# Layer 0's output projection: six pairs of tiles by seven half-size block products, the residual by accumulating DMAs, and copies put behind stores

## The chip, the cores and the metric

The kernel runs on one core of a Trainium2 chip. A core has TensorE (PE, matmuls; PEld is its weight load), VectorE (DVE), ScalarE (ACT), GpSimd (POOL) and SyncE (SP, which here only starts DMAs); ACT and POOL can start DMAs too, and each engine takes its instructions in order. Sixteen DMA engines move the data. The metric is the device time of one execution in microseconds (us), lower is better.

## The reference

Two layers of a diffusion backbone work on 2304 tokens of 1024 features: 256 context tokens (two tiles of 128) and 2048 latent ones (sixteen tiles). Layer 0 is even (latent attention and gated linear attention side by side), layer 1 is odd (neighbourhood attention on a grid of width 64). Cut to what matters here:

```python
def even_mixer(...):
    ...
    def readout(a, b, za, zb):
        a = a.reshape(bsz, n, A_WIDTH) * jax.nn.silu(za)
        b = rms_norm(b, gla_gain).reshape(bsz, n, B_WIDTH) * jax.nn.silu(zb)
        return jnp.dot(jnp.concatenate([a, b], axis=-1), w_out)

def reference(...):
    for i in range(DEPTH):
        shift, scale, gate = modulation(c, ada_w[i], ada_b[i])
        h = rms_norm(x, norm_g[i]) * (1 + scale) + shift
        ...
        y, yc = even_mixer(...) if i % 2 == 0 else odd_mixer(...)
        x = x + gate * y
        if update_ctx:
            cx = cx + c_gate * yc
    return x
```

The change touches `jnp.dot(..., w_out)` of layer 0, a product of 2304 x 1024 by 1024 x 1024, and the sum `x + gate * y` behind it. All is fp32.

## The kernel before

An fp32 product is made of three matmuls of rounded halves: each operand is split into a high part (rounded to the matmul's type fp32r, by ACT) and a low part (the rest, by DVE), and high·high, high·low and low·high are added up in PSUM. A matmul has a 128x128 block of activations as its stationary operand and a 128x512 block of weights as its moving one; a tile of 128 tokens against 1024x1024 weights takes 8 blocks of k, 2 halves of the columns and 3 products, 48 matmuls.

The stages, with their stretches in the trace of before: even_latent and even_rest (0 to 1100 us; layer 0's input products, even_rest storing its columns as Un and zaT with POOL's DMAs), even_mix (1100 to 1895 us; attention and gated linear attention, their readout stored as RT, transposed), layer 0's output projection (1895 to 2093), odd_qk and odd_vz (2093 to 3004; layer 1's input products, cell by cell: a cell is a tile t against 512 columns j of w_od), layer 1's attention (3004 to 3400), and layer 1's output projection (to the end). Tiles of SBUF come from pools with a fixed number of buffers per tag (`bufs`), and an instruction that writes a buffer waits for the last reader of its former content. The order on each engine is set by a scheduling layer from the data's dependences and the order of the code; `issue_after(x)` puts what stands in it behind x on its engine.

The projection is `project`, called by even_mix. For each tile it loads RT (pr, 512 KB) and xin (px, 512 KB) by SP (`project_load`), splits pr into prh and prl (`project_split`), runs 48 matmuls into two banks pj (`project_steps`), multiplies each bank by the gate (DVE, py, L1284), adds the residual on POOL (px<-py,px, L1288), and stores the tile to x1 in DRAM by SP. The weights w_out0 lie in SBUF, split, in places that earlier stages have left: D0 to D13, gu, gqt, gkt, gkT, gat, tri, woh/wol and gG. Between tiles, the generator `ahead` makes steps of the next stage: the splits of w_od's columns j = 2 and 3 (w0h/w0l, w1h/w1l, `od_steps`) and the preps of tiles 0 and 1 of layer 1, which read x1, normalise and transpose it (8 PE transposes, L339) and scale it to hT.

odd_qk goes over the cells in the order of `cells`: the first two tiles together (0,2), (1,2), (0,3), (1,3), then tile by tile; tile t + 2's prep is made when a tile has had its last cell. The weights of j = 0 and 1 (w2h/w2l and w3h/w3l, L106 and L391) are loaded and split beside the first four cells. odd_vz stores silu(z) as z1 (z<-ozt, ACT's DMA, L1453) and copies x1's latent tiles to the output in DRAM (out_dram<-x, 16 copies of 512 KB, ACT's queue, L1455); since these wait for x1 alone, the schedule had them earlier, from 1941.7 to 2098.0 us.

Layer 1's output projection (L1826 on) has the scheme that the change brings to layer 0: tiles 0 to 3 plain, then six pairs by seven products of half size (`seven`, matmuls at L1940), the results added to the output by POOL's accumulating DMAs (L1960).

Of the kernel before, what the change touches and what calls it, by code (L numbers as in the profile page):

```python
# [88 lines left out]
class Kern:  # L89
# [236 lines left out]
    def transposed(self, t, src, pp, tag, xp=None):  # L326

        nc, sp = self.nc, self.prp
        x = self.tl(xp or sp, [P, D], "x", bufs=1)
# [44 lines left out]
    def split_steps(self, dst, key, wp, src, K, cols, tag, step, rows=None, stage=None, place=None):  # L374
# [8 lines left out]
        for k0 in range(0, K, step):  # L383
            s = slice(k0, min(k0 + step, K))
            for c0 in range(0, cols, width):
# [3 lines left out]
                if rows is None:  # L389
                    self.act(hi[:, s, c], w[:])  # L390
                    nc.vector.tensor_tensor(out=lo[:, s, c], in0=w[:], in1=hi[:, s, c], op=ALU.subtract)  # L391
                    continue
# [8 lines left out]
    def even_latent(self, ws, wrest, kept):  # L401
# [6 lines left out]
        with ExitStack() as es:  # L408
# [3 lines left out]
            with ExitStack() as es2:  # L412
                st = self.pool(es2, "adaS", side="left", reuse_waits="tile")
                rows = self.transposed(0, self.i["xin"], pp, px, st)
# [192 lines left out]
    def even_rest(self, ws, win, hT):  # L607
        nc = self.nc
        self.zaT = self.scr("zaT", (4, P, T), F32)
        with ExitStack() as es:  # L610
# [5 lines left out]
            def cell(t, j):  # L616
# [547 lines left out]
    def even_mix(self, e1, win, hT):  # L1164
        nc = self.nc
        self.RT = self.scr("RT", (KD, P, T), F32)
        self.x1 = self.scr("x1", (T, D), F32)
        with ExitStack() as es:
            with ExitStack() as esa:
# [31 lines left out]
                def side():  # L1201
# [11 lines left out]
                    pre[0] = self.project_load(self.RT, 0, self.i["xin"], ld)  # L1213
                    yield "unit"
                    yield "unit"
                    r, x = pre[0]
                    hi, lo = self.tl(ld, [P, KD, P], "prh", F32R, bufs=1), self.tl(ld, [P, KD, P], "px", F32R)
                    self.project_split(r[:], hi[:], lo[:])
                    pre[0] = hi, lo, r, x
# [9 lines left out]
            def ahead():  # L1229
                for j in (2, 3):  # L1230
                    yield from self.od_steps(win, j, ws)
                for t in range(2):
                    hT[t] = self.prep(1, t, self.x1, pp, ("pj", 4))
                    yield
                    yield

            u = 2 * KD - 1
            self.split_unit(w, u, self.load_unit(u, self.tl(sp, [P, 512], "py")), [self.tl(g1, [P, 512], "gG", F32R, bufs=2)[:] for _ in range(2)])
            gate = [self.gate_load(0, c, self.tl(sp, [P, D], f"gate{c}", bufs=1)[:]) for c in range(2)]
            self.project(self.RT, range(NT), self.i["xin"], self.x1, w, sp, pp, pre["ld"], pre, gate, ahead())  # L1240
# [17 lines left out]
    def project_load(self, RT, t, xsrc, ld):  # L1258
# [3 lines left out]
        x = self.tl(ld, [P, D], "px")  # L1262
        self.nc.sync.dma_start(x[:], xsrc[t * P : t * P + P, :])
        return r, x
# [5 lines left out]
    def project_steps(self, hi, lo, x, g, w, bank, y, dst, split=KD):  # L1270
# [4 lines left out]
        for n, k0, k1 in runs:  # L1275
            c = slice(n * 512, n * 512 + 512)
            if k0 == 0:
                ps[n] = bank()
            yield from self.mm3_steps(ps[n][:], (lambda k: hi[:, k, :], lambda k: lo[:, k, :]),
                                      (lambda k: w[k, n][0][:, 0, :], lambda k: w[k, n][1][:, 0, :]), range(k0, k1), k0 == 0, k1 == KD)  # L1280
# [10 lines left out]

    def gate_load(self, l, c, g):
# [3 lines left out]
    def project(self, RT, tiles, xsrc, dst, w, sp, pp, ld, pre, gate, ahead):  # L1296

        for t in tiles:
            if t in pre:
                hi, lo, r, x = pre.pop(t)  # L1300
            else:
                hi, lo = [self.tl(sp, [P, KD, P], "pr" + c, F32R)[:] for c in "hl"]
                r, x = self.project_load(RT, t, xsrc, ld)
                self.project_split(r[:], hi, lo)
# [798 lines left out]
```

## Time and profile before

| what | us |
|---|---|
| time, median of three runs (lowest to highest) | 3562.49 (3561.96 to 3566.05) |
| profiled execution, its own time | 3569.04 |
| its span | 3567.2 |
| output projection of layer 0, first to last matmul | 1895.11 to 2092.97 |
| start of odd_qk, to its first full stretch | 2092.97 to 2135.64 |
| TensorE busy, share of the span | 3465.4, 97% |
| mean granted clock of TensorE | 0.987 |

A row of the timeline or of a chain is start, length, engine and operation, `out<-in` by the program's tile names. In grouped rows a bar stands ahead of busy time, mean duration in ns, and the idle time just before with what ended it. A window's row gives, for each engine, busy us and in brackets the number of instructions. Matmuls overlap: one lasts 0.39 us and they start 0.227 us apart.

### The profile page before, as it was taken

How to read it: one execution, taken by the hardware profiler on the slowest of the kernel's cores; microseconds unless marked ns; L12 is line 12 of the kernel's file. 1: busy time of each engine (PE TensorE's matmuls, PEld its weight loads, DVE VectorE, ACT ScalarE, POOL GpSimd, SP SyncE). 2: the span in 40 equal slices, each digit the busy share in tenths (PEclk: the TensorE clock that was granted, in tenths of full speed). 3: DMA queues.
4: the chain of work that ended last, by engine and by line, in shares of the span. 5: the costliest groups of instructions: out<-in, count | busy, mean ns of one | idle time of the engine just before them, and what ended most of it. 6: DMA issues, size and time to landing. Idle time of an engine off the chain costs nothing.

```text
span 3567.2 us, 54003 instructions
## 1 busy us (share of the span) xinstructions
PE 3465.4 (97%) x19532; PEld 2680.1 (75%) x19532; DVE 2400.1 (67%) x4709; ACT 1419.3 (40%) x2562; POOL 1248.8 (35%) x1382
## 2 busy tenths in 40 slices
PE   7999998999999999999999999999899999999999
PEld 6888987888896666665557878888788887555577
DVE  4677655888885777768874345545577784666775
ACT  5454552111113455446653124444422223555532
POOL 1333431100101333322212233333334443888842
PEclk9999999999999999999999999999999999999999
DMA  7555554222215242334526654445744447888675
GB/s 252 150 155 161 148 144 137 72 87 76 86 52 153 64 132 79 110 111 139 169 82 210 212 174 134 139 144 167 234 146 127 145 121 189 214 218 223 188 213 92
DMA packets 377292, 521.52 MB, mean 146 GB/s; under 512 B 34153, under 2 KB 253753, under 8 KB 370866
## 3 DMA queue, kind: packets, MB, share of 16 engines
q1 hardware_dynamic: 329762, 418.42, 40.7%
q0 software_dynamic: 24096, 63.26, 6.8%
q10 hardware_dynamic: 23168, 36.38, 2.9%
q8 instruction: 155, 2.54, 0.3%
q14 instruction: 111, 0.91, 0.1%
HBM read 338.62 MB, written 187.69 MB: 148 GB/s over the span
## 4 chain that ended last, share of the span: by engine, by line
PE 80%; DMA 7%; DVE 6%; ACT 2%; POOL 2%; issue 2%; SPq 1%; DVEq 0%; ACTq 0%; POOLq 0%
PE st L1130 10%; PE gm L129 10%; PE gm L130 10%; PE gm L131 10%; PE av L1040 7%; PE mx L660 4%; PE o L1624 2%; PE st L1590 2%; DMA wraw<-w_od 2%; PE pj L129 2%; PE pj L131 2%; PE pj L130 2%; PE o L1940 2%; DMA adaw<-ada_w 1%; PE st L1940 1%
## 5 line engine op out<-in xcount | busy, mean ns | idle before, releaser
L661 DVE TENSOR_REDUCE mm<-mx 128x1 f32<-128x512 f32 (+1 forms) x656 | 388.6, 629 | 82.3 <-PE mx L660 75.2
L106 ACT ACTIVATE apt<-st 128x1024 f32<-128x1024 f32 (+1 forms) x296 | 300.2, 1015 | 308.6 <-PE st L1130 293.7
L1137 DVE TENSOR_TENSOR acc<-acc,apt 128x1024 f32<-128x1024 f32 x256 | 340.6, 1330 | 81.0 <-ACT apt L106 61.6
L1130 PE MATMUL st<-aq,akh 64*128 64x512 f32 x1728 | 313.9, 410 | 1.1 <-ACT apt L106 0.8
L1040 PE MATMUL av<-apt,av 128*64 128x512 f32 x1152 | 265.8, 598 | 0.0
L1749 DVE TENSOR_TENSOR opt<-st,tab 128x64 f32<-128x64 f32 (+10 forms) x576 | 144.5, 318 | 144.3 <-PE st L1591 66.4
L660 PE MATMUL mx<-mk,mq 96*128 96x512 f32 (+1 forms) x656 | 236.0, 373 | 2.1 <-DMA mq<-QC 1.4
L1630 POOL TENSOR_TENSOR oacc<-oacc,opt 128x576 f32<-128x576 f32 (+5 forms) x192 | 223.3, 1190 | 38.5 <-DVE oacc L1614 13.8
L1130 PE MATMUL st<-aq,akl 64*128 64x512 f32 (+1 forms) x1152 | 231.8, 392 | 0.0
L1130 PEld LDWEIGHTS st<-aq,akh 64*128 64x128 f32 x1728 | 154.1, 186 | 83.0 <-ACT apt L106 29.1
L106 ACT ACTIVATE u<-gm 128x352 f32<-128x352 f32 (+1 forms) x140 | 68.5, 497 | 368.3 <-PE gm L131 208.3
L1507 DVE CUSTOM_DVE_ANT_1 mx<-mx,mtab 128x217 f32<-128x217 f32 (+12 forms) x576 | 184.0, 338 | 37.5 <-PE mx L1501 28.2
L1040 PEld LDWEIGHTS av<-apt,av 128*64 128x64 f32 x1152 | 76.3, 136 | 135.2 <-issue 134.2
L106 ACT ACTIVATE opt<-opt 128x930 f32<-128x930 f32 (+8 forms) x130 | 104.4, 805 | 110.0 <-DVE opt L1749 106.4
L660 PEld LDWEIGHTS mx<-mk,mq 96*128 96x128 f32 x656 | 121.2, 188 | 14.9 <-DVE mm L661 1.9
L1130 PEld LDWEIGHTS st<-aq,akl 64*128 64x128 f32 (+1 forms) x1152 | 113.0, 185 | 23.1
L106 ACT ACTIVATE x<-px,modB,modA 128x128 f32<-128x128 f32 x272 | 99.5, 468 | 59.5 <-PE px L339 56.5
L129 PE MATMUL gm<-w1h,hhi 128*128 128x512 f32 x288 | 116.2, 404 | 6.9 <-ACT onat L106 6.9
L129 PE MATMUL gm<-w0h,hhi 128*128 128x512 f32 x288 | 116.5, 404 | 1.9 <-DVE hhi L351 1.9
L130 PE MATMUL gm<-w1l,hhi 128*128 128x512 f32 x288 | 115.1, 400 | 0.0
L210 POOL TENSOR_TENSOR oss<-oss,mhalf 128x8 f32<-128x8 f32 x68 | 113.2, 1665 | 5.1
L130 PE MATMUL gm<-w0l,hhi 128*128 128x512 f32 x288 | 114.6, 398 | 0.0
(579 smaller groups left out, 9700.9 us busy)
## 6 DMA issues: line engine op xcount, KB each, us to landing
q<-Q SPq DMA_DIRECT2D x48, 512.0 KB
H<-x ACTq DMA_DIRECT2D x36, 512.0 KB
adaw<-ada_w SPq DMA_DIRECT2D x64, 256.0 KB
x<-H SPq DMA_DIRECT2D x32, 512.0 KB
wraw<-w_od SPq DMA_DIRECT2D x64, 256.0 KB
K1t<-okt POOLq DMA_DIRECT2D x32, 512.0 KB, 7.3
kt<-K1t SPq DMA_DIRECT2D x32, 512.0 KB
mtab<-rpb_q SPq DMA_DIRECT2D x16, 899.0 KB
```

The costliest lines, as they stand in the source:

```text
L106: return self.nc.scalar.activation(out, in_, func, **kw)
L129: self.nc.tensor.matmul(out, lh(k), rh(k), start=start and j == 0, stop=False)
L130: self.nc.tensor.matmul(out, lh(k), rl(k), start=False, stop=False)
L131: yield self.nc.tensor.matmul(out, ll(k), rh(k), start=False, stop=stop and j == n - 1)
L660: mm = nc.tensor.matmul(ps[:, :w], q[:A_QK, (t % 6) * P : (t % 6) * P + P], k[:A_QK, k0 : k0 + w], start=True, stop=True)
L661: nc.vector.tensor_reduce(out=m[:, t, n : n + 1], in_=ps[:, :w], axis=AX.X, op=ALU.max)
L1040: mm = nc.tensor.matmul(O[j, nb][i * 64 : i * 64 + 64, :w], V[j, kt // TT][:, kt % TT, i * 64 : i * 64 + 64], pts[:, i, :w], start=n == 0, ...
L1130: mm = nc.tensor.matmul(ps[:, o // 64, :w], k[o : o + r, kb, kq], Q[o : o + r, qb, :w], start=m == 0, stop=m == 4)
L1137: added = nc.vector.tensor_tensor(out=acc[:, :, :w], in0=a[:, :, :w], in1=pts[:, :, :w], op=ALU.add)
L1507: nc.vector.tensor_tensor_reduce(out=s, in0=s, in1=tb[:, ri : ri + rn, ci : ci + cn], scale=1.0, scalar=-3e38, op0=ALU.add, op1=ALU.max, a ...
L1630: self.psum = nc.gpsimd.tensor_tensor(out=a, in0=a, in1=pts[:, :, a0 - r0 : a1 - r0, :], op=ALU.add)
L1749: bias = nc.vector.tensor_tensor(out=pt[:, d[0], d[1]], in0=ps[:, d[0], d[1]], in1=tabs[j][i][:, ri : ri + rn, ci : ci + cn], op=ALU.add)
```

## The change

It has five parts.

1. **Products.** `even_output` takes the place of `project`. Tiles 0 to 3 are plain. Tiles 4 to 15 go in six pairs: the two tiles' 256 x 1024 by 1024 x 1024 product is split in halves of rows, k and columns, and seven half-size products (`seven`; each 4 blocks of k by 3, 12 matmuls, 84 a pair where two plain tiles have 96) stand for eight. Their activations are A (first tile), B (second), and sums of half tiles S and S4 (`pair_operands`, DVE); their weights are blocks B11, B21, B22 as they are, and four sums T1 to T4 (`weight_sums`). For these, w_out0 is loaded once more (eight loads of 512 KB), and sixteen differences and twelve splits are made during tiles 1 to 3, into places of prep tiles and of w0 and w1. T4 goes into the place of the plain weights of k = 0 to 3, right half; under tile 16 those are loaded again and split, and tiles 16 and 17, plain, take k from 4 to 7 first. Three results of a pair are made by DVE from PSUM and one of three ACT copies (py) and the gate, the fourth from PSUM and the gate.
2. **Residual.** x1 is filled with xin ahead of time, by 18 copies of 512 KB from DRAM to DRAM on POOL's queue in even_rest, each behind a store of Un. The projection's results are added to it by 36 accumulating DMAs of 256 KB on POOL's queue. The px loads, POOL's adds and SP's stores of x1 go.
3. **Copies of x1 to the output.** Each is now ordered behind the store of z1 for the same tile (j = 7) in odd_vz, on ACT's queue.
4. **odd_qk.** `cells` has one tile in its first group: (0,2), (0,3), (1,2), (1,3), (2,2) and so on. The splits of w_od are ordered behind a DVE result, `self.done` (in the projection the last result, in odd_qk the last onat). The prep of tile 0 stands in the last pair, that of tile 1 in tile 17.
5. **Shared code.** Layer 1's output uses `weight_sums`, `pair_operands`, `seven` and `pair_result` too; S4 is there made in ra in place of zb.

Three places of the engines' order. First DVE in the projection. Before, a result (py, L1284) follows a result, with one split per tile (prl):

```order
L1284 TENSOR_TENSOR py_18674<-pj_18649,gate_3291_18424 128x512
L1284 TENSOR_TENSOR py_18702<-pj_18677,gate_3291_18424 128x512
L1268 TENSOR_TENSOR prl_18790<-pr_18791,prh_18789 128x1024
L1284 TENSOR_TENSOR py_18747<-pj_18722,gate_3291_18424 128x512
L1284 TENSOR_TENSOR py_18775<-pj_18750,gate_3291_18424 128x512
L1268 TENSOR_TENSOR prl_18863<-pr_18864,prh_18862 128x1024
```

Now a pair has, from the second half of one to the next one's first product results (L393: split of the next stage's weights; L1259: splits of operands; L1350 to L1352: results; L1303: sums of half tiles):

```order
L1259 TENSOR_TENSOR prl_18746<-x_18749,prh_18745 128x1024
L1350 TENSOR_TENSOR py_18890<-pu_18778,gate_3290_18440 128x512
L393 TENSOR_TENSOR w0l_18896<-wraw_18897,w0h_18895 128x512
L393 TENSOR_TENSOR w0l_18896<-wraw_18901,w0h_18895 128x512
L1259 TENSOR_TENSOR prl_18748<-pr_18776,prh_18747 128x1024
L1259 TENSOR_TENSOR prh_18742<-pr_18774,prh_18742 128x512
L1351 TENSOR_TENSOR py_18924<-pj_18911,py_18924 128x512
L1352 TENSOR_TENSOR py_18924<-py_18924,gate_3290_18440 128x512
L1259 TENSOR_TENSOR px_18744<-pr_18905,px_18743 128x1024
L1351 TENSOR_TENSOR py_18938<-pu_18909,py_18938 128x512
```

The results of a pair stand between splits and sums for the pair to come, and each waits for a product. Next ACT at the projection's end, before (prh: a tile's high part; osq: squares for a norm in odd_qk):

```order
L106 ACTIVATE prh_19657<-pr_19659 128x1024
L1455 DMA out_dram<-x 16x8192 x2
L106 ACTIVATE w2h_19752<-wraw_19754 128x512
L106 ACTIVATE w2h_19752<-wraw_19758 128x512
L106 ACTIVATE w2h_19752<-wraw_19774 128x512
L1455 DMA out_dram<-x 16x8192
L106 ACTIVATE osq_19782<-gm_19739 128x512
L106 ACTIVATE w2h_19752<-wraw_19778 128x512
```

and now (D: the plain weights put back under T4's place; hlo,ssx: squares of tile 1 of layer 1; x<-pj: its modulation):

```order
L106 ACTIVATE prh_19660<-pr_19662 128x1024
L106 ACTIVATE D_3163_17628<-px_19489 128x512
L106 ACTIVATE w1h_19583<-wraw_19649 128x512
L106 ACTIVATE w1h_19583<-wraw_19653 128x512
L106 ACTIVATE x_19679<-pj_19688,modB_8_72,modA_6_70 128x128 x4
L106 ACTIVATE x_19679<-pj_19689,modB_8_72,modA_6_70 128x128 x4
L354 DMA H<-x_19679 128x1024
L106 ACTIVATE w2h_19784<-wraw_19786 128x512
L106 ACTIVATE w2h_19784<-wraw_19790 128x512
```

The copies to the output have left this stretch, and ahead of the first split of w2 stand the splits of w1, the plain weights and tile 1's prep. Last POOL, at the hand-over from projection to odd_qk, before:

```order
L1288 TENSOR_TENSOR px_19596<-py_19625,px_19596 128x512
L1288 TENSOR_TENSOR px_19596<-py_19653,px_19596 128x512
L1288 TENSOR_TENSOR px_19661<-py_19690,px_19661 128x512
L1288 TENSOR_TENSOR px_19661<-py_19718,px_19661 128x512
L208 TENSOR_SCALAR oss_19784<-oss_19784 128x8
L210 TENSOR_TENSOR oss_19784<-oss_19784,mhalf_65 128x8
```

and now (x<-py: an accumulating DMA into x1):

```order
L1420 DMA x<-py_19456 128x512
L208 TENSOR_SCALAR ssx_19683<-ssx_19683 128x1
L210 TENSOR_TENSOR ssx_19683<-ssx_19683,mhalf_65 128x1
L1420 DMA x<-py_19553 128x512
L1277 DMA x<-py_19613 128x512
L1277 DMA x<-py_19657 128x512
L1277 DMA x<-py_19723 128x512
L1277 DMA x<-py_19751 128x512
L208 TENSOR_SCALAR oss_19816<-oss_19816 128x8
L210 TENSOR_TENSOR oss_19816<-oss_19816,mhalf_65 128x8
```

DMAs stand where the adds stood, and tile 1's prep (ssx) lies between those of the last pair. The diff, its part on layer 1's output and some hunks of helpers left out:

```diff
-    def cells(tiles, js, keep=lambda t, j: True, edge=2):
+    def cells(tiles, js, keep=lambda t, j: True, head=2):
         n = len(tiles)
-        groups = [tiles[:edge]] + [[t] for t in tiles[edge : n - edge]] + [tiles[n - edge :]]
+        groups = [tiles[:head]] + [[t] for t in tiles[head : n - 2]] + [tiles[n - 2 :]]
...
-                    self.act(hi[:, s, c], w[:])
-                    nc.vector.tensor_tensor(out=lo[:, s, c], in0=w[:], in1=hi[:, s, c], op=ALU.subtract)
+                    with self.tc.issue_after(after().ins) if after else ExitStack():
+                        self.act(hi[:, s, c], w[:])
+                        nc.vector.tensor_tensor(out=lo[:, s, c], in0=w[:], in1=hi[:, s, c], op=ALU.subtract)
...
-                    nc.gpsimd.dma_start(self.Un[t, :, 1056:], u[:])
+                    st = nc.gpsimd.dma_start(self.Un[t, :, 1056:], u[:])
+                    with self.tc.issue_after(st.ins):
+                        nc.gpsimd.dma_start(self.x1[t * P : t * P + P, :], self.i["xin"][t * P : t * P + P, :])
...
+    H4 = KD // 2
+    HALF = slice(0, 512), slice(512, D)
+    def weight_sums(self, a, b, t1, t2, t3):
+        dif = lambda o, x, y: self.nc.vector.tensor_tensor(out=o, in0=x, in1=y, op=ALU.subtract)
+        u, v = [[x[:, c] for c in self.HALF] for x in (a, b)]
+        dif(u[0], u[1], u[0])
+        self.project_split(u[0], *t1)
+        dif(u[1], v[1], u[1])
+        dif(v[1], v[1], u[0])
+        self.project_split(v[1], *t2)
+        yield
+        dif(v[0], v[0], v[1])
+        self.project_split(u[1], *t3)
+        yield
+    def pair_operands(self, ra, rb, s, h):
+        lo, hi = slice(0, self.H4), slice(self.H4, KD)
+        tt = lambda o, x, y, op: self.nc.vector.tensor_tensor(out=o, in0=x, in1=y, op=op)
+        def sums():
+            tt(s[:, lo, :], rb[:, lo, :], rb[:, hi, :], ALU.add)
+            tt(s[:, hi, :], s[:, lo, :], ra[:, lo, :], ALU.subtract)
+            self.project_split(s, *h["S"])
+        def more():
+            tt(rb[:, lo, :], ra[:, lo, :], rb[:, lo, :], ALU.subtract)
+            tt(ra[:, hi, :], ra[:, hi, :], s[:, hi, :], ALU.subtract)
+            self.project_split(ra[:, hi, :], *h["S4"])
+        return [lambda: self.project_split(ra, *h["A"]), sums, more, lambda: self.project_split(rb, *h["B"])]
+    def seven(self, h, w, U, V, W, copy, result):
+        part = lambda x, n: [y[:, n * self.H4 : n * self.H4 + self.H4, :] for y in x]
+        def prod(ps, A, Bk, start):
+            with self.tc.issue_after(self.mm.ins) if self.mm else ExitStack():
+                for k in range(self.H4):
+                    for n, (x, y) in enumerate(((A[0], Bk[k][0]), (A[0], Bk[k][1]), (A[1], Bk[k][0]))):
+                        self.mm = self.nc.tensor.matmul(ps, x[:, k, :], y, start=start and k == 0 and n == 0,
+                                                        stop=k == self.H4 - 1 and n == 2, skip_group_check=True)
+        prod(U, part(h["A"], 0), w["B11"], True)
+        s1 = copy(U, 0)
+        prod(V, part(h["S"], 0), w["T1"], True)
+        s5 = copy(V, 1)
+        prod(U, part(h["S"], 1), w["T2"], False)
+        u2 = copy(U, 2)
+        prod(W, part(h["A"], 1), w["B21"], True)
+        self.done = result(W, s1, 0, 0)
+        yield
+        prod(U, part(h["B"], 0), w["T3"], False)
+        self.done = result(U, s5, 1, 1)
+        yield
+        prod(V, h["S4"], w["B22"], False)
+        self.done = result(V, u2, 0, 1)
+        yield
+        prod(U, part(h["B"], 1), w["T4"], False)
+        self.done = result(U, None, 1, 0)
+        yield
+    def pair_result(self, ps, x, gate, y):
+        if x is None:
+            x = y()
+            return x, self.nc.vector.tensor_tensor(out=x[:], in0=ps, in1=gate, op=ALU.mult)
+        self.nc.vector.tensor_tensor(out=x[:], in0=ps, in1=x[:], op=ALU.add)
+        return x, self.nc.vector.tensor_tensor(out=x[:], in0=x[:], in1=gate, op=ALU.mult)
...
+    def even_output(self, w, sp, pp, pre, win, hT, ws):
+        nc, h4, ld, prp = self.nc, self.H4, pre["ld"], self.prp
+        PLAIN = 4
+        gates = [self.tl(sp, [P, D], "gate0", bufs=1), self.tl(prp, [P, D], "x", bufs=1)]
...
+        def weights7():
+            raw = [self.tl(ws[0], [P, h4, D], "w0" + z, bufs=1) for z in "hl"]
+            for k in range(h4):
+                for n, x in enumerate(raw):
+                    nc.sync.dma_start(x[:, k, :], self.i["w_out0"][:, n * h4 + k, :])
+            yield
+            t1 = [[self.tl(prp, [P, 2, 512], "h" + z, F32R, bufs=2) for _ in range(2)] for z in ("hi", "lo")]
+            w7["T1"] = [[x[k // 2][:, k % 2, :] for x in t1] for k in range(h4)]
+            for t, z in (("T2", "h"), ("T3", "l")):
+                x = self.tl(ws[0], [P, KD, 512], "w1" + z, F32R, bufs=1)
+                w7[t] = [[x[:, k, :], x[:, h4 + k, :]] for k in range(h4)]
+            for k in range(h4):
+                yield from self.weight_sums(raw[0][:, k, :], raw[1][:, k, :], *(w7[t][k] for t in ("T1", "T2", "T3")))
+            late.extend((raw[1][:, k, self.HALF[0]], w7["T4"][k]) for k in range(h4))
...
+        s4 = self.tl(ld, [P, KD, P], "prh", F32R, bufs=1)
+        h7 = {"A": [self.tl(ld, [P, KD, P], "px", F32R)[:] for _ in range(2)], "S": parts(), "B": parts(),
+              "S4": [s4[:, :h4, :], s4[:, h4:, :]]}
+        scratch = self.tl(prp, [P, KD, P], "x", bufs=1)
+        def pair(t):
+            ra, rb = [self.project_load(self.RT, t + n, ld) for n in range(2)]
+            return self.pair_operands(ra[:], rb[:], scratch[:], h7)
...
+        def result(t):
+            def f(ps, x, row, n):
+                x, done = self.pair_result(ps, x, gates[0][:, self.HALF[n]], y)
+                nc.gpsimd.dma_start(self.x1[(t + row) * P : (t + row) * P + P, self.HALF[n]], x[:], accum_op=ALU.add)
+                return done
+            return f
+        ops, self.mm = pair(PLAIN), None
+        for n in range(4):
+            ops[n]()
+            if n == 1:
+                for x, place in late:
+                    self.project_split(x, *place)
+        ahead = self.od_steps(win, 2, ws, lambda: self.done)
+        for t in range(PLAIN, NT - 2, 2):
+            end = t + 4 == NT
+            if not end:
+                ops = pair(t + 2)
+            U = self.tl(pp, [P, 512], "pu", bufs=2)
+            for n, _ in enumerate(self.seven(h7, w7, U[:], bank()[:], bank()[:], copy, result(t))):
+                if not end:
+                    with self.tc.issue_after(self.done.ins):
+                        ops[n]()
+                    if n == 3:
+                        next(ahead, None)
+                elif n == 1:
+                    back = [self.tl(ld, [P, KD, P], "px")[:].rearrange("p k t -> p (k t)") for _ in range(2)]
+                    for k in range(h4):
+                        nc.sync.dma_start(back[k // 2][:, self.HALF[k % 2]], self.i["w_out0"][:, k, self.HALF[1]])
+                    hT[0] = self.prep(1, 0, self.x1, pp, ("pj", 4))
+        for _ in ahead:
+            pass
+        ahead = self.od_steps(win, 3, ws, lambda: self.done)
+        for t in range(NT - 2, NT):
+            hi, lo = parts()
+            self.act(hi, (r := self.project_load(self.RT, t, ld))[:])
+            self.done = nc.vector.tensor_tensor(out=lo, in0=r[:], in1=hi, op=ALU.subtract)
+            if t == NT - 2:
+                for k in range(h4):
+                    self.project_split(back[k // 2][:, self.HALF[k % 2]], *w7["T4"][k])
+            for n, _ in enumerate(self.project_steps(hi, lo, None, gates[0], w, bank, y, self.x1[t * P : t * P + P, :],
+                                                        [*range(h4, KD), *range(h4)])):
+                if n % 4 == 3:
+                    next(ahead, None)
+                if n == 3 and t == NT - 1:
+                    hT[1] = self.prep(1, 1, self.x1, pp, ("pj", 4))
...
-            cells = self.cells(list(range(NT)), (2, 3, 0, 1), lambda t, j: j > 1 or t >= NCT) + [(NT - 2, 4), (NT - 1, 4)]
+            cells = self.cells(list(range(NT)), (2, 3, 0, 1), lambda t, j: j > 1 or t >= NCT, 1) + [(NT - 2, 4), (NT - 1, 4)]
...
-                nc.scalar.dma_start(self.z1[(j - 6) * 4 : (j - 6) * 4 + 4, :, o : o + P].rearrange("j p t -> p j t"), z[:])
+                st = nc.scalar.dma_start(self.z1[(j - 6) * 4 : (j - 6) * 4 + 4, :, o : o + P].rearrange("j p t -> p j t"), z[:])
                 if j == 7:
-                    nc.scalar.dma_start(self.out[o : o + P, :], self.x1[CTX + o : CTX + o + P, :])
+                    with self.tc.issue_after(st.ins):
+                        nc.scalar.dma_start(self.out[o : o + P, :], self.x1[CTX + o : CTX + o + P, :])
```

More of the change, by code (lines that the diff above doesn't have):

```diff
@@ L372, in split_w, with split_steps @@
         return d[0]
-    def split_steps(self, dst, key, wp, src, K, cols, tag, step, rows=None, stage=None, place=None):
+    def split_steps(self, dst, key, wp, src, K, cols, tag, step, rows=None, stage=None, place=None, after=None):
         nc = self.nc
@@ L1892, in two @@
                 return [by_k(x[:, i].rearrange("p r c -> p (r c)")) for i in range(2)]
[L1894 to L1903 removed]
+            s4 = whole(ones["kt"][1])
```

231 lines of the change are left out of this document (85 added, 146 removed).

## The prediction

> **What bounds the kernel now.** I read the page's head first, then each stage by windows, then the chain of waits where TensorE (PE) falls short of full.
>
> ```profile
> span 3567.2 us, 54003 instructions
> PE 3465.4 (97%) x19532; PEld 2680.1 (75%) x19532; DVE 2400.1 (67%) x4709; ACT 1419.3 (40%) x2562; POOL 1248.8 (35%) x1382
> q10 hardware_dynamic: 23168, 36.38, 2.9%
> ```
>
> PE is busy 97% of the span, so a matmul taken out of a dense stretch is worth its interval, until something else ends last there. The last line is a DMA queue: 36.38 MB in 2.9% of 3567 us, 103 us, or 352 GB/s with all 16 engines at work; a copy of 512 KB (0.524 MB) takes about 1.5 us of all of them. The profiled execution took 3569.04 us (1.84 beside the span), 6.55 over the median of the three runs, 3562.49; the sum is a difference against it, and I carry it to the median.
>
> Next the windows: layer 0's output projection (operations on tile pj alone), the start of odd_qk behind it (all operations), even_rest, its end and the end of odd_vz, to which copies move, and two pairs of layer 1, which use the seven-product scheme already. The columns are length, busy time of PE, weight loads, DVE, ACT and POOL (as far as each took part), granted clock, DMA share, GB/s.
>
> ```profile
> 1895.11:2092.97 197.86, 197.86 (x880) 163.74 (x880) 24.05 (x35) 5.78 (x16) 1.00 0.65 217
> ...
> 2092.97:2135.64 42.67, 38.77 (x169) 31.43 (x168) 22.45 (x36) 19.17 (x37) 19.05 (x26) 0.92 0.65 204
> ...
> 550.00:1090.00 540.00, 534.08 (x2752) 470.57 (x2751) 434.71 (x729) 76.07 (x133) 53.55 (x92) 1.00 0.29 86
> ...
> 1090.00:1100.00 10.00, 8.54 (x49) 6.73 (x49) 1.38 (x2) 2.60 (x4) 6.25 (x11) 1.00 1.04 306
> 2980.00:3000.00 20.00, 20.00 (x93) 16.45 (x92) 1.82 (x2) 5.22 (x7) 1.19 (x2) 1.00 1.04 284
> 3503.45:3522.92 19.47, 19.47 (x86) 15.77 (x84) 12.36 (x17) 5.50 (x7) 6.56 (x6) 1.00 0.56 105
> 3522.92:3542.38 19.46, 19.46 (x86) 15.78 (x84) 11.25 (x16) 5.50 (x7) 3.44 (x5) 1.00 0.41 55
> ```
>
> The projection is full: 197.86 of 197.86 us, at clock 1.00. Its 880 are 864 matmuls (18 tiles, 2 halves, 8 blocks, 3 products) and 16 transposes, which stand in the chain as two groups:
>
> ```profile
> 1993.32 0.87 PE pj L339 x8
> 2016.02 0.87 PE pj L339 x8
> ```
>
> So one matmul is worth (197.86 − 1.74)/864 = 0.2270 us, a pair of plain tiles, 96 of them, 21.79 us, and a tile 10.9 us.
>
> **The products.** Six pairs of 84 matmuls stand for six of 96: 72 go. At 0.2270 that is 16.3 us (19.07 a pair). Layer 1's pairs of the same scheme last 19.46 and leave PE no gap: 6 × (21.79 − 19.46) = 14.0. Between the two I take 19.2 a pair: 6 × 2.59 = **−15.5**, bounds −16.3 and −14.0.
>
> Is a pair dense here too? Layer 1's rows give DVE 12.36 us at most for the same result, sum and split operations. Layer 0 adds two weight splits (w0l) to four of the pairs, and nothing on POOL, whose adds go:
>
> ```profile
> L391 DVE TENSOR_TENSOR w0l<-wraw,w0h 128x512 fp32r<-128x512 f32 x8 | 5.9, 770 | 6.6 <-ACT w0h L106 6.6
> L1268 DVE TENSOR_TENSOR prl<-pr,prh x17: 1216/2342/2357, 1900.1 to 2072.3; 128x1024 fp32r<-128x1024 f32 x17
> L1284 DVE TENSOR_TENSOR py<-pj,gate 128x512 f32<-128x512 f32 x36 | 24.7, 690 | 97.0 <-PE pj L131 94.5 <-DMA gate<-gates 2.5
> L1288 POOL TENSOR_TENSOR px<-py,px 128x512 f32<-128x512 f32 x36 | 47.3, 1315 | 144.7 <-DVE py L1284 128.3 <-DMA px<-xin 6.6 <-DMA wraw<-w_od 5.5
> ```
>
> DVE: 12.36 + 2 × 0.77 = 13.9 of 19.2 us. But its order matters. Counted from a pair's first matmul, with 12 matmuls a product (2.74 us): the last result of the pair before at 0.2 to 0.9, w0l twice to 2.4, the low part of B to 3.6 and of S4 to 4.3. These free the two pr buffers, so the loads of the pair after next start at about 3.7 and 4.3. Their first reader is ACT's high part of A, behind the fourth product, at 11.0; so a load has 7.3 us for nothing. The nearest rows are a 512 KB transfer and the accumulating stores, issue to landing:
>
> ```profile
> K1t<-okt POOLq DMA_DIRECT2D x32, 512.0 KB, 7.3
> ...
> DMA to landing us min/median/max: 3.6/4.3/8.8
> ```
>
> From 11.0 on DVE has A's low part, two results, four sums and S's low part: 1.22 × 2 + 0.69 × 8 and the waits between, ending near 20.4; PE asks for S's low part in the next pair's second product, at 21.9. That is 1.5 us of slack beside a load that is just in time, so 0 a pair. The 36 accumulating stores take the place of 9.4 MB loaded and 9.4 MB stored, and 47.3 us of adds leave POOL: off the path, nothing gained.
>
> **The first pair.** The eight 512 KB loads of weights (4.2 MB, 12 us at 352 GB/s) lie beside tile 0. Sixteen differences and twelve splits, 28 × 0.69 = 19.3 us of DVE, with six results (4.1), two tiles' splits (2.4) and the first pair's operands (about 6) make 32 us, over tiles 0 to 3, 43.6 us. Layer 1's first pair, with the same list, did make PE wait (the chip's answer on PE's waits there):
>
> ```profile
> PE st L1940 <- DVE oacc L1268: 1.8, 1, 1.8
> PE st L1940 <- ACT oacc L106: 1.4, 1, 1.4
> ```
>
> Bounds 0 and +3.2; with 11 us of room I take **+0.5**.
>
> **The end of the projection.** Eight T4 blocks are made late or restored (4 × 256 KB loads, 4 splits) under tile 16, and both preps of odd_qk's first tiles now stand in the last pair and tile 17, where ACT and DVE also have the w1 splits. By the order, one result of the last pair comes behind two casts and three splits: two bank evictions of 0.69 and those against 2.74 us of a product. I take **+1**, bounds 0 and +3.
>
> **The start of odd_qk.** Its chain of waits before (start, length), with two rows of the timeline between:
>
> ```profile
> 2095.33 1.68 ACT L106 ACTIVATE w2h<-wraw 128x512 fp32r<-128x512 f32 x3 [23.10 <-POOL px L1288]
> ...
> 2119.40 1.94 PE L339 MATMUL px<-ident,x 128*128 128x128 f32 x8 [3.38 <-DVE x L336]
> ```
> ```profile
> 2096.72 2.92 DMA wraw<-w_od
> ...
> 2101.05 4.15 DMA wraw<-w_od
> ...
> 2118.51 0.74 DVE x L336
> ...
> 2122.94 0.55 PE gm L129
> 2123.49 0.43 PE gm L130
> ...
> 2126.05 0.23 PE gm L131
> ```
>
> Some 7 us are lost here already: PE stood 42.67 − 38.77 = 3.9 us (3.38 for tile 2's x), eight transposes took 1.94 where 0.87 is usual, and from 2122.94 to 2126.05 matmuls ran at 0.43, eight of them, 1.6 us over, with four slow transposes ahead. ACT's first w2 split waited 2.4 us behind the projection's end for POOL's last add. Now it waits for the last accumulating stores: 0.7 (result) + 0.9 (issue) + 4.3 (landing), about 6 us, so 3.5 later. Against that, tile 2's prep is released one cell (24 matmuls, 5.5 us) sooner, since tile 0 is done after two cells, and the out copies on ACT's queue are gone from there. I take **0**, bounds −5 (the loss of 7 mostly gone) and +3 (the 3.5 in full).
>
> The slow matmuls stand behind an idle stretch of 3.38 us, at a granted clock of 0.92 over the window. [...]
>
> **The copies.** 18 copies of xin to x1 stand on POOL's queue behind Un's stores; DMA has 0.29 of its time taken there, so 16 cost nothing (POOL is busy 53.55 of 540 us). The last two fall on 1090 to 1100, where the share is 1.04 and PE is short of 1.46 us; behind it a load waits long, as two do behind odd_vz:
>
> ```profile
> 1103.26 9.78 DMA gn<-gla_norm
> ```
> ```profile
> 3010.12 13.06 DMA q<-Q
> ...
> 3034.96 7.61 DMA kt<-K1t
> ```
>
> Two copies are 3 us of all engines, bounds 0 and +3, and I take **+1** since other loads of the queue aren't on the chain. The 16 copies of x1 to out now stand behind z's stores on ACT's queue over odd_vz, the last two at 2985 to 3000, with the share at 1.04 already; 3 us more in front of Q and K1t: bounds 0 and +6 (each of both waits longer by 3), and I take **+1.5**.
>
> [...]
>
> Layer 1's code is rewritten with one operand in another buffer; the order of its first pair's loads shifts a little: 0, bounds −1 and +1.
>
> Sum: −15.5 + 0.5 + 1 + 0 + 1 + 1.5 = **−11.5**: 3557.5 for the profiled execution, **3551.0** against the median. The best bounds make −22.3, the worst +5.2 (3540 to 3568).
>
> **Rivals.** (1) The gain goes to the hand-overs: +3 at the end, +3 at 1100, +4 to +6 at 3010, +2 at odd_qk: −15.5 + 13 = −2.5, **3560**. For it: both places are at 1.04. Against: PE itself is full until 3000.
>
> (2) Slower: pr's loads. With two buffers a late load delays A's high part, and with it all that DVE does behind it; beyond 1.5 us of slack each us costs six. Slower by 7.1 us needs (7.1 + 15.5 − 4)/6 = 3.1 us a pair, a load of 7.3 + 1.5 + 3.1 = 11.9 us. At 12.8 us: six times 4.0, **3575**. For it: q's 13.06. Against: 7.3 is the median, and the projection's share of 0.65 falls by px's loads, x1's stores and the out copies.
>
> (3) odd_qk's 7 us go mostly: −15.5 + 4 − 5 = −16.5, **3546**, or 3542 with the copies free.
>
> DVE as the bound of the pairs is no rival: with the three long splits at the 2342 ns that they took beside POOL's adds it comes to 13.9 + 3.4 = 17.3 us of 19.2.
>
> **Chances.** A measurement tells about 0.2%, 7.1 us: under 3555.4 is faster, over 3569.6 slower. Forecast (3547 to 3555) 0.58, rival 3 0.11: faster 0.69. Rival 1 0.20: same. Rival 2 0.11: slower. The range 3542 to 3566 leaves out the end of rival 3 and rival 2.
>
> **What would show it.** Right: the projection 180 to 184 us long from its first matmul to its last, PE without gaps in its pairs, 84 matmuls each; odd_qk's first 43 us as long as before; q's wait near 3010 longer by 1 or 2 us. Wrong: PE waiting in each pair for prh, px or prl splits with pr's load as their releaser (rival 2); gaps over 3 us at 1100 or 3040 (rival 1); w2l waits on PE near 2115.

## The result and the profile after

The changed kernel takes 3557.32 us (median of 22 runs, 3549.78 to 3563.25), the kernel before 3565.9 beside it (22 runs, 3560.01 to 3573.55): a ratio of 0.9975, 95% interval 0.9968 to 0.9982, or 8.9 us less. Forecast were 11.5 us less. The page of the changed kernel, profiled at 3556.47 us:

```profile
span 3554.5 us, 54024 instructions
PE 3452.1 (97%) x19460; PEld 2667.5 (75%) x19460; DVE 2442.8 (69%) x4799; ACT 1450.2 (41%) x2612; POOL 1241.9 (35%) x1400
```

PE has 72 matmuls fewer and is as full as before. The two spans differ by 12.7 us, more than the medians: single executions of one kernel lie some 10 us apart, so stages are compared below over all the profiles taken. Windows of all operations, first before (even_mix from its first st<-aq to the projection; the first 126 us of odd_qk, to the first K1t store of okt), then after (the same with the projection and one pair between):

```profile
1100.50:1895.11 794.61, 789.39 (x5409) 480.20 (x5409) 596.47 (x653) 432.02 (x727) 216.36 (x198) 1.00 0.36 109
2092.97:2218.60 125.63, 121.73 (x574) 100.20 (x573) 66.19 (x104) 60.21 (x116) 49.50 (x64) 0.97 0.48 149
```
```profile
1100.50:1896.76 796.26, 788.85 (x5408) 479.65 (x5408) 595.78 (x653) 432.04 (x727) 215.97 (x200) 1.00 0.36 109
1896.76:2080.97 184.21, 183.82 (x810) 150.17 (x809) 120.23 (x172) 68.27 (x106) 33.75 (x40) 1.00 0.74 170
1959.76:1979.11 19.35, 19.35 (x86) 15.77 (x84) 12.46 (x18) 6.56 (x9) 3.47 (x5) 1.00 0.70 136
2080.97:2209.70 128.73, 121.34 (x574) 99.57 (x573) 65.60 (x104) 59.85 (x116) 48.43 (x64) 0.97 0.49 142
```

The projection is 184.21 us long where it was 197.86: 13.7 less, with PE idle for 0.4 us. A pair, from the first matmul of one to that of the next, takes 19.35 us without a gap, in all five intervals between the six pairs. Its 84 matmuls start 0.2303 us apart in the mean: those with T1 to T3 as moving operand (tiles w1h, w1l, hhi, hlo) 0.233 to 0.234 us, those into pu from D (T4) or gu 0.227, the plain tiles' figure; why, no run shows. The other stages are longer: even_mix by 1.7 us, odd_qk's start by 3.1. PE's waits at these two places, before and after the change:

```profile
PE gl L730 <- DVE rT L723: 2.5, 1, 2.5
...
PE px L339 <- DVE x L336: 3.4, 1, 3.4
PE tp L1365 <- DVE onat L1357: 0.5, 1, 0.5
```
```profile
PE gl L735 <- DVE rT L728: 4.3, 1, 4.3
...
PE tp L1519 <- DVE onat L1511: 4.7, 2, 2.7
PE gm L129 <- DVE hhi L352: 2.7, 1, 2.7
```

### The profile page after: what moved, and what is told of

It is laid out like the page before. It is cut to its first block, busy times and chain, and to the rows that moved or that the text cites. A ratio compares the mean times of both kernels' runs of the same rounds, so it can differ in the third digit from the quotient of the medians.

```text
span 3554.5 us, 54024 instructions
## 1 busy us (share of the span) xinstructions
PE 3452.1 (97%) x19460; PEld 2667.5 (75%) x19460; DVE 2442.8 (69%) x4799; ACT 1450.2 (41%) x2612; POOL 1241.9 (35%) x1400
## 5 line engine op out<-in xcount | busy, mean ns | idle before, releaser
L1662 DVE CUSTOM_DVE_ANT_1 mx<-mx,mtab 128x217 f32<-128x217 f32 (+12 forms) x576 | 184.0, 338 | 38.8 <-PE mx L1656 29.7
L131 PE MATMUL gm<-w1h,hlo 128*128 128x512 f32 x288 | 114.7, 398 | 0.0
```

The lines of the kernel that those rows point to most:

```text
L131: yield self.nc.tensor.matmul(out, ll(k), rh(k), start=False, stop=stop and j == n - 1)
L1662: nc.vector.tensor_tensor_reduce(out=s, in0=s, in1=tb[:, ri : ri + rn, ci : ci + cn], scale=1.0, scalar=-3e38, op0=ALU.add, op1=ALU.max, a ...
```

## Experiments

Each run is compared with the kernel before, on the same chip; one thousandth is 3.6 us. Four marks were read off every profile: even_mix (first st<-aq to the projection's first matmul), odd_qk's start (as above), the attention's start (odd_vz's last transposes to POOL's first oacc sum), and the end (last o<-q,oacc matmul to the span's end).

| kernel | ratio (95% interval) | even_mix | odd_qk | attention | end |
|---|---|---|---|---|---|
| before | 1 | 794.6 | 125.6 | 28.4 | 8.4 |
| changed | 0.9975 (0.9968 to 0.9982) | 796.3 | 128.7 | 30.1 | 5.6 |
| e1_plain | 1.0017 (1.0003 to 1.0030) | 798.6 | 127.2 | 30.3 | 5.2 |
| e2_fill_early | 0.9966 (0.9954 to 0.9979) | 794.9 | 127.6 | 30.3 | 5.4 |
| e3_out_early | 0.9972 (0.9961 to 0.9983) | 792.4 | 128.9 | 28.5 | 5.5 |
| e4_w2_place | 0.9976 (0.9965 to 0.9987) | 798.3 | 126.6 | 35.8 | 5.5 |
| f1_layer1_code | 0.9999 (0.9989 to 1.0008) | 791.3 | 124.0 | 30.6 | 8.4 |
| f2_odd_qk | 0.9990 (0.9978 to 1.0002) | 795.1 | 131.2 | 29.9 | 5.4 |
| f3_three | 0.9960 (0.9946 to 0.9973) | 791.6 | 128.9 | 34.0 | 5.4 |
| f4_copies_only | 1.0002 (0.9993 to 1.0012) | 790.9 | 126.2 | 29.7 | 8.4 |
| g2_last_results | 0.9973 (0.9961 to 0.9985) | 797.9 | 128.0 | 29.8 | 5.4 |
| g1_three | 0.9966 (0.9956 to 0.9977) | 792.8 | 129.0 | 29.0 | 5.5 |
| h1_early_old | 0.9977 (0.9968 to 0.9986) | 798.2 | 129.8 | 29.5 | 5.4 |
| h2_early_old_fill | 0.9953 (0.9941 to 0.9966) | 792.8 | 129.0 | 30.2 | 5.5 |

**The products.** e1_plain runs all 18 tiles plain in the changed kernel (the next stage's splits and preps stand between tiles again, as before the change):

```diff
-        for t in range(PLAIN):
+        for t in range(NT):
...
-        ops, self.mm = pair(PLAIN), None
```

> The changed kernel with all 18 tiles plain: no pairs and no weight sums, but the residual by accumulating DMAs, the x1 copies, the copies behind the stores and the cell order of odd_qk stay. If the products carry the whole gain, as the prediction's sum had it, the projection is back at some 198 us and the time is 13 to 15 us above the changed kernel, so 4 to 7 us above the kernel before (some 3571 us where that has 3566). If the residual by DMAs gains something of its own (POOL's adds, px loads and x1 stores gone), it lies at or below the kernel before (3560 to 3566).

It is slower than before by 6.1 us (1.1 to 10.7), and 15.0 above the changed kernel (0.0042 of 3566). Its own projection:

```profile
1894.00:2095.20 201.20, 199.28 (x882) 163.62 (x881) 63.21 (x82) 37.23 (x56) 33.19 (x40) 1.00 0.59 131
```

3.3 us of the 15 are its own (PE idle for 201.20 − 199.28 = 1.9 us, and 1.4 us longer busy), which leaves about 12 for the products by the times, some 5 either way by the two intervals; the windows above give 13.7. Without the products the other parts together gain nothing: of the loss of 6.1 us, 3.3 lie in the projection and 2.8 elsewhere. The residual by DMAs was not tested by itself.

**The fill of x1.** e2_fill_early issues each copy two tiles sooner:

```diff
-                        nc.gpsimd.dma_start(self.x1[t * P : t * P + P, :], self.i["xin"][t * P : t * P + P, :])
+                        for f in [fill.pop() for _ in range(min(len(fill), 3 if len(fill) == NT else 1))]:
+                            nc.gpsimd.dma_start(self.x1[f * P : f * P + P, :], self.i["xin"][f * P : f * P + P, :])
```

> The changed kernel with the copies of xin to x1 two tiles earlier (three behind the first store of Un, then one each, none behind the last two). In the trace the first product of gla waited 4.3 us for DVE after the change and 2.5 before. If the last two copies cause that, this wait is 2.5 again and the time falls by 1 to 2 us; if it is the scatter of that hand-over, wait and time stay within 1 us of the changed kernel.

e2 alone does not settle it: it lies 3.2 us below the changed kernel, within the intervals, and the wait that its expectation names is 3.2 us. All profiles together tell more. In the column even_mix three kernels without a fill have 791 to 795 us (mean 792.3), seven with the fill's end at the hand-over 792 to 799 (mean 796.7), four with the earlier fill, whose last copy starts near 1040 us in place of 1100, 792 to 795 (mean 793.0). So even_mix pays 4.4 us, and 3.7 of them go when the last copies come two tiles sooner; the 3.7 compare kernels that have the same other parts, singly or together, and the other 0.7 do not. The times agree: the mean ratio of those four is 0.9961, that of changed, e3, e4, g2 and h1 0.9975, so 4.7 us, some 3 either way by their intervals. PE was idle for 794.61 − 789.39 = 5.2 us of this stage before and for 7.4 after; with the earlier fill (h2) for 3.0:

```profile
1096.90:1889.70 792.80, 789.77 (x5409) 479.69 (x5409) 596.23 (x653) 432.03 (x727) 214.85 (x198) 1.00 0.36 108
```

PE's wait for rT hangs on a small load. On DVE rT stands behind gw, which waits for a load of 2 KB; SP starts that load behind all its earlier ones, 24.4 to 25.7 us after the first st<-aq without a fill, 25.6 to 27.6 with the fill's end at the hand-over, 22.2 to 26.4 with the earlier one. DVE's wait before, after and in h2 (where PE does not wait for rT at all):

```profile
DVE gw L898 <- DMA gw<-gw: 9.6, 1, 9.6
```
```profile
DVE gw L903 <- DMA gw<-gw: 11.4, 1, 11.4
```
```profile
DVE gw L905 <- DMA gw<-gw: 4.6, 1, 4.6
```

In the means of the three groups PE waits 1.9, 3.5 and 1.1 us for rT, and single profiles scatter as much (e3 has 1.1 with the fill's end at the hand-over). So of the 4.4 us, 1.6 are this wait, PE's other idle time adds 0.3, and 2.5 are longer busy time of PE in this stage, which no row explains.

**The copies to the output.** e3_out_early shifts them by two stores; f4_copies_only puts the unchanged kernel's copies behind z1's stores:

```diff
+                    with self.tc.issue_after(st.ins):
+                        for f in [copies.pop(0) * P for _ in range(min(len(copies), 3 if len(copies) == NT - NCT else 1))]:
+                            nc.scalar.dma_start(self.out[f : f + P, :], self.x1[CTX + f : CTX + f + P, :])
```

> The changed kernel with the copies of x1 to the output two stores earlier, so that none lies at the end of odd_vz. The prediction put +1.5 us (0 to +6) on the last two: if they do delay Q and K1t, the time falls by 1 to 2 us and the wait for q near 3005 us is shorter by 1 to 3 us; the rival is that these loads are late for reasons of their own (share over 1.0 there before the change too), and nothing moves by more than 1 us.

> The kernel before with its 16 copies of x1 to the output ordered behind z1's stores, and nothing else changed. The prediction's sum has +1.5 us at the start of the attention and something off odd_qk's start, where the copies leave ACT's queue (five wraw waits of 2.6 to 5.3 us stand in the chain there): -2 to +2. If the copies cost time wherever odd_vz's own transfers are, as the changed kernel's odd stages suggest (904 us from the first cell to the last against 899), it is 2 to 5 us slower than the kernel before.

e3 lies 1.1 us below the changed kernel and f4 0.7 above the kernel before, both within their intervals. The attention's start is 29.5 to 30.3 us with the copies at odd_vz's end (eight kernels, mean 30.0) and 28.4 to 30.6 without (before, f1, e3, g1; mean 29.1): some 0.9 us, which is no more than the scatter. SP waits for loads of q there for 5.7 us before, 5.4 after and 4.7 in e3, so the expected change of 1 to 3 us is not seen.

**The start of odd_qk.** e4_w2_place exchanges the places of w2 and w3 in SBUF:

```diff
         ws.append(self.pool(e1, "owT", side="left", reuse_waits="tile"))
+        for n in (3, 2):
+            for z in "hl":
+                self.tl(ws[1], [P, KD, 512], f"w{n}{z}", F32R, bufs=1)
```

> The changed kernel with the buffers of w3 and w2 exchanged in SBUF, so that w2 no longer lies on py and its first split doesn't wait for the last accumulating DMAs (it waits for a matmul of the last tile's last bank); w3 lies there in its place. If the late w2 splits cost the 3 us that odd_qk's start lost after the change, w2's first split starts about 6 us earlier, PE's waits for onat and hhi there (2.7 + 2.7 + 1.9 us in the changed kernel) shrink and the time falls by 3 to 5 us. If the loss is in the chain of norms and preps (POOL's power, tile 2's prep) or in the cell order, it stays within 1 us.

The time stays, and a wait has moved: the attention's start grew to 35.8 us (34.0 in f3, which has this edit too). SP starts the attention's fourth load of q at odd_vz's last transposes there (0.1 us behind them in e4, 0.2 ahead in f3), where the other twelve kernels have it 4.4 to 6.1 us ahead of them. w3's place is used to the last cells, and the attention's first loads now lie in it. The wait of SP's queue for matmuls of odd_vz fits that, 9.9 us at once against 4.5, but it is no proof by itself: e3 has 10.5 us in two waits and a start of 28.5. First e4, then the changed kernel:

```profile
SPq L111 <- PE gm L131: 9.9, 1, 9.9
```
```profile
SPq L111 <- PE gm L131: 4.5, 1, 4.5
```

That the time stays all the same is not explained; e4's stretch from there to the last o<-q,oacc is the shortest of all (534.7 us), f3's is not (539.4). g2_last_results takes w2's wait away without the exchange: tile 17's results stand in S4's buffer.

```diff
+        spare = self.tl(ld, [P, KD, P], "prh", bufs=1)[:].rearrange("p k t -> p (k t)")
+        last = [spare[:, c] for c in self.HALF]
...
-  ... w, bank, y, self.x1[...]
+  ... w, bank, y if t < NT - 1 else lambda: last.pop(0), self.x1[...]
```

> The changed kernel with the two results of tile 17 in a buffer of S4's (under w3's place) in place of py's, so that w2's first split waits for DVE's last result and no more for the last accumulating DMAs, while w2 and w3 keep their places. By the exchange of w2 and w3, odd_qk's start (first cell to the last K1t store of oqh) went from 48.2 to 44.7 us, but the attention's first POOL sum came 35.8 and 34.0 us behind odd_vz's last transposes, where all others have 28.4 to 30.6. If that is the price of w3's place under the attention's first loads, it is 28 to 31 here, w2's first split starts 1 us behind the projection's end in place of 5.7, and the time falls by 2 to 4 us against the changed kernel. If the start of odd_qk isn't set by w2, nothing falls by more than 1 us.

ACT's first split of w2 in the changed kernel, behind 11.26 us of waiting that the accumulating DMA ended, and in g2, released by DVE's last result (the projection ends at 2080.97 and 2081.0):

```profile
2086.69 1.68 ACT L106 ACTIVATE w2h<-wraw 128x512 fp32r<-128x512 f32 x3 [11.26 <-DMA x<-py]
```
```profile
2081.92 1.67 ACT L106 ACTIVATE w2h<-wraw 128x512 fp32r<-128x512 f32 x3 [6.47 <-DVE prh L1275]
```

The split starts 4.8 us earlier, the attention's start is 29.8 again, and yet odd_qk's start is 128.0 us and the time the same to 0.7 us (by its interval, to 5 us). So with the new cell order the late w2 isn't what sets the 128. f2_odd_qk puts the old cell order back and no longer orders the splits of w2 and w3 behind onat; h1_early_old does that with the early w2:

```diff
-            ... lambda t, j: j > 1 or t >= NCT, 1) + [(NT - 2, 4), (NT - 1, 4)]
+            ... lambda t, j: j > 1 or t >= NCT) + [(NT - 2, 4), (NT - 1, 4)]
-            self.ahead += [self.od_steps(win, j, ws, lambda: self.done) for j in (0, 1)]
+            self.ahead += [self.od_steps(win, j, ws) for j in (0, 1)]
```

> The changed kernel with odd_qk as it was: two tiles in the first group of cells, the splits of w2 and w3 not ordered behind onat. If the new cell order and split order cost what odd_qk's start lost (48.2 us from the first cell to the last K1t store of oqh there, against 45.1), that stretch is 45 us again and the time falls by 3 us; if they make up for the later w2, as the prediction took it, the stretch grows by 2 to 4 us and so does the time.

> Tile 17's results in S4's buffer (so w2's first split comes early), and odd_qk as before the change (two tiles in the first group of cells, splits not ordered behind onat). From odd_qk's first matmul to the first K1t store of okt the traces have 124.0 to 126.2 us in the kernels with the old order and no accumulating DMAs, 131.2 with the old order and the late w2, 127.2 to 128.9 with the new order and the late w2, 126.6 to 129.0 with the new order and an early w2. If the late w2 costs 6 us and the new order takes back 3 of them and costs 3 of its own, it is 124 to 126 here and the time is 2 to 4 us below the changed kernel. If something else of the changed kernel's end of projection costs it (preps in its last tiles, loads), it stays at 128 to 131.

With the old order and the late w2 it is 131.2 us and the time 5 us higher than the changed kernel's (the intervals touch, and 1.9 of it lie in the projection, 186.1 us long); with the old order and the early w2 129.8 and 129.0; with the new order 128.1 as the mean of four kernels with the late and of four with the early w2; without any accumulating DMAs 125.3 (three kernels). As far as single profiles tell, the late w2 costs some 2 us with the old order and nothing with the new one. The other 2.8 us are in all kernels with the accumulating DMAs, e1_plain's too (1.9 there), but these differ from the three in the fill, the preps and the order of splits as well, and the cause is open. What the traces show is where PE waits: for onat, whose chain runs through ACT's squares, which stand behind w3 splits waiting for their loads, and POOL's power, behind four K1t stores (g2):

```profile
2097.89 1.46 POOL L1554 DMA_DIRECT2D K1t<-oqh  x2 [1.41 <-ACT oqh L106]
2099.52 1.23 POOL L1554 DMA_DIRECT2D K1t<-oql  x2 [0.16 <-issue]
...
2101.10 2.01 POOL L210 TENSOR_TENSOR oss<-oss,mhalf 128x8 f32<-128x8 f32 x1
```

**Layer 1's code** alone, in the kernel before (the functions of the changed kernel, nothing else):

> The kernel before with layer 1's output code of the changed kernel alone (shared functions, S4 made in ra in place of zb). In the changed kernel, from the last of the odd attention's own products (st<-oacc,mtwos) to the first o<-q,oacc the trace shows 41.1 us where before had 43.0, and from the last matmul to the span's end 5.6 us where before had 8.4. If both are the rewritten code's, this kernel is 3 to 5 us faster than the kernel before; if they are scatter of single executions, as the prediction's 0 (bounds -1 and +1) says, it is within 1.5 us of it.

The time changes by 0.4 us, within 4. The shorter end isn't this code's, since f1 has 8.4 us too. The other stretch that the expectation names (last st<-oacc,mtwos to first o<-q,oacc) is 41.4 us in f1, near the changed kernel's 41.1 and not the 43.0 of before; f4, without this code, has 43.4, and of ten further kernels with it nine have 39.7 to 41.0 and f3 43.6. So some 2 us there seem to be this code's, and f1's time is too coarse to tell.

**Together.** f3_three has both shifts of copies and the exchanged places, g1_three both shifts and g2's edit, h2_early_old_fill the earlier fill, g2's edit and the old cell order.

> The changed kernel with three edits at once: the fill of x1 two tiles earlier, the copies to the output two stores earlier, and w3's buffers exchanged with w2's. If each place of contention is worth what the stages showed (1 to 2, 1 to 2 and 2 to 3.5 us), the time is 4 to 7 us below the changed kernel, some 3551 us where the kernel before has 3566; if the waits move on to the next stage, it is within 2 us of the changed kernel.

> That edit with both shifts of copies (x1's fill two tiles earlier, the output's copies two stores earlier). If the three add up, and no wait is given back at the attention's start as with the exchanged places, it is 6 to 9 us below the changed kernel and 2 to 4 below the kernel with the exchange (ratio to the kernel before 0.994 to 0.996); if the gains lie within the scatter of the hand-overs, it is like the changed kernel to 3 us (0.9965 to 0.998).

> The same, with x1's fill two tiles earlier. From the attention's first matmul in even_mix to the projection's first, kernels without the fill have 790.9 to 794.6 us (mean 792), with the fill at the end of even_rest 792.4 to 798.6 (six, mean 796), with the earlier fill 791.6 to 794.9 (three, mean 793). If both theories hold, 791 to 795 there and 124 to 126 in odd_qk, and the time is 5 to 7 us below the changed kernel (ratio to the kernel before 0.9955 to 0.996); if only the fill counts, 3 to 4 below it.

All four kernels with the earlier fill are below the changed kernel by 3 to 8 us: f3 by 5, as expected, g1 by 3 and not 6 to 9, h2 by 8, over its 5 to 7. h2 has the lowest ratio, 16.8 us below the kernel before (12 to 21), at 3550.1 us, but with odd_qk at 129.0, not the 124 to 126 that were expected: only the fill is shown to count, and the kernels with it don't differ among themselves beyond their intervals.

## Why the prediction was right, step by step

- **The products** (−15.5, and +0.5 and +1 at both ends, −14.0): measured −13.7. A pair takes 19.35 us (taken: 19.2), 6 × (21.79 − 19.35) = 14.6; the bound of −16.3 needed 0.227 us a matmul with every weight, and those with T1 to T3 took 0.233 to 0.234. The weight sums were in time, and the projection's end kept PE waiting for 0.4 us in place of 1. No pair waited for a load: rival 2 did not come.
- **The fill's last two copies** (+1, bounds 0 and +3): mis-sized. They cost 4.4 us, outside the bounds. The prediction kept this term small since other loads of the queue aren't on the chain; the load of gw is, and 1.9 of the 4.4 us are idle time of PE, most of it the wait for rT behind that load. The other 2.5, longer busy time, are open.
- **odd_qk's start** (0, bounds −5 and +3): measured +2.8, at the edge. That the new order pays for the later w2 is what f2 suggests; that nothing else came was wrong, and the rest is open.
- **The copies to the output** (+1.5): measured some 0.9, and 0.7 for the whole time (−2.5 to +4.3) where they are moved alone; neither is clear of the scatter, and SP's waits for q, which were to grow, did not (5.7 and 5.4 us).
- **Layer 1's code** (0, bounds −1 and +1): −0.4, within 4; the traces suggest −2.
- **Not in the sum**: the end of the program, −2.9 us (below).

The terms measured make −13.7 + 4.4 + 2.8 + 0.9 − 2.9 = −8.5, and the time shows −8.9 (−11.4 to −6.4). That is closer than the terms can claim. They leave out two stretches: from odd_qk's first K1t store of okt to odd_vz's last transposes the eleven kernels with the changed projection are 1.2 us longer in the mean than the three with the old one, and from the attention's start to the last matmul 3.1 us shorter, with which the sum would be −10.4. Layer 1's code may be 2 of the 3.1; the rest of these two was not tested.

The mechanism held: 72 matmuls fewer were worth 13.7 us (72 intervals of 0.227 are 16.3), and the hand-overs took some of it back. That the total came so near the forecast is partly luck. The fill took 3.4 us more and odd_qk 2.8 more than forecast, and the program's end and the stretch before it gave back about as much, which the sum didn't have. The forecast's −11.5 lies just outside the interval. The 3557.32 us lie within the range of 3542 to 3566, above the 3547 to 3555 named as the forecast; 3.4 us of that is the kernel before itself, 3565.9 in 22 runs and 3562.49 in the three that the forecast started from. Rival 1, the hand-overs, was half true: they gave back some 8 us, not 13, and its sign came, a gap over 3 us near 1100 (4.3, where before has 2.5). In rival 3 the 3542 takes back 4 us of the other terms, where the copies' own are 2.5 (3543.5).

## What to carry to other kernels

Here 72 matmuls taken out of a stretch where PE had no gap were worth 13.7 us, 0.19 us each where their interval is 0.227; pairs of the same shape, dense at 19.46 us in layer 1 of the trace of before, foretold the 19.35 they came to. Look for what such an edit gives back at the stages' hand-overs: it was 4.4 us in even_mix and 2.8 at odd_qk's start, and at two hand-overs the DMA share stood at 1.04 before the change. Put bulk copies a few tiles ahead of such a place: moving the last ones two tiles forward was worth some 4 us. Look there for a small load that stands late in a queue, with a result on the chain behind it. And ask, of a buffer that is moved to end one wait, who loads into its old and its new place next: the exchange of w2 and w3 made the attention's start 4 to 6 us longer.

## What was not expected of the hardware

The span does not end with the last transfer, and what follows differs between programs. From the last matmul's start to the span's end it is 8.4 us in all three kernels with the old projection (before, f1, f4), and 5.2 to 5.6 in the eleven others. The DMA engines' busy tenths in the last 9 us, in 40 slices, before, in f1 and after:

```profile
DMA  9600009957699559993200000000000000000000
```
```profile
DMA  9100009579889767983000000000000000000000
```
```profile
DMA  9962209469999900009927969887985310000000
```

After the last packet 20 slices (4.5 us) pass before, and 7 (1.6 us) after the change, with the same last instructions. The trace shows what ends last: a DRAIN of POOL on the kernel's last line, which starts with POOL's last DMA. POOL has three of them there, and the rows give the shortest, median and longest in ns; the longest is meant. First before, then after:

```profile
L2097 POOLq DRAIN  x3: 40/93/8238, 3558.2 to 3567.0; - x3
```
```profile
L2181 POOLq DRAIN  x3: 46/102/4846, 3548.3 to 3554.2; - x3
```

It takes 8.2 us in the three kernels with the old projection and 4.6 to 4.9 in the eleven others. Before, it ends at 3566.5 us, 2.9 after SP has done its last waits, and so sets the end; after the change it is over at 3553.1, 0.6 ahead of SP. Why it is shorter no run shows; in the profiles 2.9 us of the gain come from it.
